# First FFN of a two-layer encoder: three pairs on unnormalised tokens, then three Strassen groups on normalised ones

## The chip, the cores and the metric

The kernel runs on one core of a Trainium2 chip. Five engines work beside each other, each with its own queue of instructions that it takes in order: TensorE (PE, matmuls and transposes; PEld is its loading of the stationary operand), VectorE (DVE), ScalarE (ACT), GpSimd (POOL) and SyncE (SP, which issues the DMAs). An instruction waits at the head of its queue until what it reads has been written and what it overwrites has been read. The metric is the device time of one execution in microseconds; the median of several runs is compared.

## The reference

Two layers. In each, a first FFN, a token mixer and a second FFN, each with a norm before it and one behind it. There are 256 tokens of width 1024; the FFN's hidden width is 2816. All arrays are float32. The change concerns the first FFN of the first layer alone:

```python
def rms_norm(x, g):
    xf = x.astype(jnp.float32)
    xf = xf * lax.rsqrt(jnp.mean(xf * xf, axis=-1, keepdims=True) + NORM_EPS)
    return (xf * g.astype(jnp.float32)).astype(x.dtype)

def swiglu(h, w_up, w_down):
    a, b = jnp.split(h @ w_up, 2, axis=-1)
    return (jax.nn.silu(a) * b) @ w_down

for l in range(DEPTH):
    h = rms_norm(x, ffn1_pre_g[l])
    x = x + 0.5 * rms_norm(swiglu(h, ffn1_w_up[l], ffn1_w_down[l]), ffn1_post_g[l])
    ...
```

## The kernel before

**Numbers.** Each float32 operand is held as two tiles of type float32r, a high part and the rest. ACT copies the high part (line 119 for weights, 164 for most others), DVE subtracts it from the original (lines 120 and 165). A product is then three matmuls, high by high, high by low and low by high (`mm3`, line 229).

**Weights.** They arrive in units of 128 x 2048 (1 MB) in the order in which they are used, through 5 buffers `raw` (line 57), and are split into 5 pairs of buffers `wh`, `wl` (line 58). `next_unit` (line 127) loads and splits; the first `FINE` = 5 units of a stage are split in four parts, later ones in two. So DVE and ACT can be some units ahead of PE, and no more.

**An FFN** (`ffn`, line 297). The hidden width is cut into 11 "pairs" of 256 gate and 256 value columns. An "up" of a pair (`up`, line 344) multiplies both halves of the tokens (c = 0, 1) by two units: 48 matmuls of 128 x 512. `swiglu` (line 334) makes silu(gate) times value from the PSUM bank; `turned` (line 320) transposes the outcome on PE and splits it into `hid`. A "down" (line 311) multiplies a pair's hidden tokens by one unit into four PSUM banks `acc`: 24 matmuls. `PLAN` (line 37) lists the order. The last three downs are done by `tail` (line 284) half by half of the tokens, so that the post-norm, the next stage's pre-norm and its transposes of the first half run beside the matmuls of the second.

**Two forms of FFN.** All FFNs but the first take normalised, transposed and split tokens, and beside them a float32 copy of the transposed tokens (`kept`, made in `pre_norm`, line 187). Their plan has six of the pairs in three "groups" (`group`, line 382): two pairs are made together by a Strassen-Winograd scheme, with 7 block products of 12 matmuls each in place of 8. It needs sums of token blocks (`token_sums`, line 372), sums of weight blocks (128 x 2048, `add` at line 364 on the `raw` tiles), 7 split units in place of 4, and sums of the products.

The first FFN of the first layer (`raw_rstd` given, line 431) has no stage before it in which x could be normalised. It takes x already transposed from memory, multiplies by the norm's gain while splitting (`first_tokens`, line 183), starts its matmuls at once, and multiplies by the reciprocal root mean square of each token where the result leaves PSUM (lines 337 and 338). Its plan has no groups: up and down of pairs 2 to 10 in turn.

**Other work in the first FFN.** `setup` (line 477) makes cosines, sines and the lambdas' sums for the mixers; `mem_scale` (line 568) takes the root mean squares of the 256 memory tokens; `mem_gain` (line 577) multiplies the transposed memory by its gain and splits it. In the first FFN these are issued behind down 2 (`n == 5`); in the other first FFN, that of layer 2, `mem_gain` is issued behind the whole plan, ahead of `tail`.

**What sets the order.** The program order sets priorities; a scheduler places each instruction into its engine's queue at compile time, ahead of earlier ones when those would wait. The order on each engine is then fixed. `issue_after` (line 137) demands an order between two instructions.

**Buffers the steps touch.** Tokens, sums of tokens and split memory share 2 tiles `xhl` (line 59); hidden and memory tiles share 12 (line 60); `s2` has 8 tiles of 512 (line 62), two of `gain` (line 63). PSUM has 4 banks `acc`, 2 `ma` and 2 `mb`; transposes go through `mb`.

Of the kernel before, what the change touches and what calls it, by code (L numbers as in the profile page):

```python
# [10 lines left out]
F32R = mybir.dt.float32r  # L11
# [6 lines left out]
P = 128  # L18
# [15 lines left out]
T_UP = 36  # L34
T_ROPE = 13
T_SC = (242, 336)
PLAN = [[(t[0], int(t[1:])) for t in plan.split()] for plan in (
    "u2 d0 u3 d1 u4 d2 u5 d3 u6 d4 u7 d5 u8 d6 u9 d7 u10",
    "u2 d0 g3 d1 d2 u5 d3 g6 d4 d5 u8 d6 g9 d7",
)]  # L40
T_KT = (200, 222)
T_DA = (186, 210, 278, 302)
T_PV = (193, 218, 285, 310)
# [8 lines left out]
def encoder_kernel(ctx, tc, x_d, xt_d, mem_d, memt_d, pos_d, w_d, gains_d, cols_d, lamv_d, poolw_d, cst_d, out_d):  # L52
# [6 lines left out]
    xts = ctx.enter_context(tc.tile_pool(name="xts", bufs=2))  # L59
# [17 lines left out]
    def t2(shape=(P, 512), dt=F32):  # L77
        return s2.tile(list(shape), dt, name="s2")
# [4 lines left out]
    x = [const.tile([P, D], F32, name=f"x{c}") for c in range(2)]  # L83
# [58 lines left out]
    def in_order(ins):  # L142
        for early, late in zip(ins, ins[1:]):
            issue_after([late], early)
# [18 lines left out]
    def split(ps, h, l):  # L163
        high = nc.scalar.copy(out=h, in_=ps)  # L164
        return high, nc.vector.tensor_tensor(out=l, in0=ps, in1=h.bitcast(F32), op=ALU.subtract)  # L165
# [131 lines left out]
    def ffn(i, xx, late, kept, g_post, finish, ahead, raw_rstd=None):  # L297
        fine[0] = FINE
        hid = {}
        acc = [[None, None], [None, None]]  # L300

        def lhs_of(c, kk, k):
            return hid[kk][0][:, c, k, :], hid[kk][1][:, c, k, :]
# [29 lines left out]

        def swiglu(p, c, ps):
            sg, hn = t2((P, S)), t2((P, S))
            if raw_rstd:
                nc.scalar.activation(out=sg, in_=ps[:, 0:S], func=AF.Silu, scale=raw_rstd[c])
                nc.vector.scalar_tensor_tensor(out=hn, in0=ps[:, S:2 * S], scalar=raw_rstd[c], in1=sg, op0=ALU.mult, op1=ALU.mult)
            else:
                nc.scalar.activation(out=sg, in_=ps[:, 0:S], func=AF.Silu)  # L340
                nc.vector.tensor_tensor(out=hn, in0=ps[:, S:2 * S], in1=sg, op=ALU.mult)  # L341
            turned(hn, c, [p])
# [20 lines left out]
        def add(out, a, b):  # L363
            nc.vector.tensor_tensor(out=out, in0=a, in1=b, op=ALU.add)  # L364

        if kept:
            sums = xts.tile([P, 2, 4 * 4, P], F32R, name="xhl")

            def summed(j):
                return lambda k: (sums[:, 0, 4 * j + k, :], sums[:, 1, 4 * j + k, :])  # L370

        def token_sums():
            a11, a12, a21, a22 = (kept[c, b] for c in range(2) for b in range(2))
            s1 = t2()
            nc.vector.tensor_tensor(out=s1, in0=a22, in1=a21, op=ALU.subtract)
            nc.vector.tensor_tensor(out=a21, in0=a11, in1=a21, op=ALU.subtract)
            nc.vector.scalar_tensor_tensor(out=a11, in0=s1, scalar=-1.0, in1=a11, op0=ALU.mult, op1=ALU.subtract)
            nc.vector.scalar_tensor_tensor(out=a12, in0=a11, scalar=-1.0, in1=a12, op0=ALU.mult, op1=ALU.subtract)
            for j, t in enumerate((s1, a11, a21, a12)):
                split(t.rearrange("p (k t) -> p k t", t=P), sums[:, 0, 4 * j:4 * j + 4, :], sums[:, 1, 4 * j:4 * j + 4, :])  # L380
# [47 lines left out]
            for c in range(2):  # L428
                swiglu(p, c, banks[c])

        if raw_rstd:
            ws = [(next_unit(), next_unit())]
            hs, ls = first_high, first_low
            (ha, la), (hb, lb), (hc, lc), (hd, ld) = (zip(*late[c, b]) for b in range(2) for c in range(2))
            in_order([*ha, *hs[0:4], *hb, *hc, hs[4], hs[5], *hd, *hs[6:8]])
            in_order([*la, *ls[0:4], *lb, *lc, ls[4], ls[5], *ld, *ls[6:8]])
            ws.append((next_unit(), next_unit()))
            for c in range(2):
                rstd_of(halves(x[c]), 1.0, None, raw_rstd[c])
            up_first(0, ws[0])  # L440
            for c in range(2):
                up(1, c, ws[1], acc_bank)
        else:
            ws = [(next_unit(), next_unit()) for _ in range(2)]
            done = []
            for c in range(2):
                for p in range(2):
                    done += up(p, c, ws[p])
            issue_after(late, done[T_UP])
            token_sums()  # L450
        for n, (what, p) in enumerate(PLAN[bool(kept)]):
            if what == "d":
                down(p)
            elif what == "u":
                up_both(p)
            else:
                group(p)
            if not kept and n == 5:
                ahead()
        if kept:  # L460
            ahead()
        todo = [(next_unit(), p) for p in range(NPR - 3, NPR)]
        return tail(acc, todo, lhs_of, 0, NPR - 1, g_post, True, finish, flush)

# [2 lines left out]
    rst = const.tile([P, 2], F32, name="rst")  # L467
# [377 lines left out]
    cur = xt_pair()  # L845
# [15 lines left out]
    late = {cb: first_tokens(*cb, xt[cb], cur) for cb in ((0, 0), (1, 0), (0, 1), (1, 1))}  # L861

    kept = None
    for i, (kind, l, row) in enumerate(stages):
        nx = {}

        def finish(c):
            if i + 1 == len(stages):
                for b in range(2):
                    fs = slice(b * 512, (b + 1) * 512)  # L870
                    nc.sync.dma_start(out=out_d[c * P:(c + 1) * P, fs], in_=x[c][:, fs])
                return []
            if c == 0:
                nx["xx"] = xt_pair()
                nx["kept"] = {} if stages[i + 1][0] == "ffn" else None
                nx["g"] = gain(stages[i + 1][1] * 10 + stages[i + 1][2])
            return pre_norm(c, halves(x[c]), nx["g"], nx["xx"], nx["kept"])()

        if kind == "ffn":
            def ahead():  # L880
                if i == 0:
                    setup()
                    mem_scale()
                if row == 0:
                    nx["mem"] = mem_gain(l)

            late = ffn(i, cur, late, kept, gain(l * 10 + row + 1), finish, ahead, [rst[:, c:c + 1] for c in range(2)] if i == 0 else None)
        else:
            late = mix(l, cur, late, mem, finish)
        cur, mem, kept = nx.get("xx"), nx.get("mem"), nx.get("kept")  # L890
# [24 lines left out]
def _pack(a, np):  # L915
    L = DEPTH
    units = []

    def cols(w, idx):
        units.append(np.ascontiguousarray(w[:, idx].reshape(KT, P, 256).transpose(1, 0, 2)).reshape(P, 2048))  # L920

    def block(w, half, col):
        units.append(np.ascontiguousarray(w[512 * half:512 * half + 512, col:col + 512].reshape(4, P, 512).transpose(1, 0, 2)).reshape(P, 2048))

    def wide(w, idx):
        both = w[:, idx]
        for half in range(2):
            block(both, half, 0)

    def rows(w, j):  # L930
        units.append(np.ascontiguousarray(w[256 * j:256 * (j + 1)].reshape(2, P, D).transpose(1, 0, 2)).reshape(P, 2048))

    def ffn(up, down, first):
        def pair(p):
            wide(up, np.r_[256 * p:256 * p + 256, D_FF + 256 * p:D_FF + 256 * p + 256])

        pair(0)
        pair(1)
        for what, p in PLAN[not first]:
            if what == "d":  # L940
                rows(down, p)
            elif what == "u":
                pair(p)
            else:
                for half, col in ((0, 0), (0, D_FF), (1, D_FF), (1, 0)):
                    block(up, half, 256 * p + col)
        for p in range(NPR - 3, NPR):
            rows(down, p)

    for l in range(L):  # L950
        ffn(a["ffn1_w_up"][l], a["ffn1_w_down"][l], l == 0)
        wi = a["w_in"][l]
        for s in (256, 768, 1280):
            wide(wi, slice(s, s + 512))
        for s in (0, 1792):
            cols(wi, slice(s, s + 256))
        wide(a["w_mem_kv"][l], slice(0, 512))
        for i in range(6):
            wide(a["w_gate"][l], slice(512 * i, 512 * i + 512))
        br = np.concatenate([a["w_br_pool"][l], a["w_br_da"][l], a["w_br_ca"][l]], axis=0)  # L960
        for i in range(2):
            wide(br, slice(512 * i, 512 * i + 512))
        for j in range(4):
            rows(a["w_out"][l], j)
        ffn(a["ffn2_w_up"][l], a["ffn2_w_down"][l], False)
    return np.stack(units)


# [39 lines left out]
```

## Time and profile before

| what | us |
|---|---|
| median of 3 runs (lowest to highest) | 1126.62 (1125.84 to 1129.25) |
| the profiled execution | 1127.05 |
| its span, first to last instruction | 1124.9 |
| busy: DVE, ACT, POOL | 893.5, 651.9, 26.1 |
| granted TensorE clock, mean | 0.997 |

Stages by the first matmul that PE takes from each: the first FFN from 6.97, its mixer from 195.2, the second FFN from 385.1, the next layer's first FFN from 565.7, its mixer from 747.2. HBM delivers 193 GB/s over the span; in the first 56 us it is 342 and 388 GB/s.

The page lists busy time for each engine, then shares of the span in 40 slices, the chain of work that ended last, and groups of instructions by source line. A row of the groups reads: line, engine, operation, tile written and tiles read, partitions x elements, type, count, then busy us, mean ns of one, and idle time of the engine ahead of them with what ended it. A row of the chain reads: start, length, engine, tile, line and count. A row of the timeline is the same with the operation named, and in brackets how long the engine had been idle and who released it. PE at 99% busy means that matmuls follow each other without a gap; it isn't a measure of how much they compute.

### The profile page before, as it was taken

What the parts mean: (1) busy time and instruction counts of PE and PEld (TensorE: products, weight loads), DVE (VectorE), ACT (ScalarE), POOL (GpSimd) and SP (SyncE); (2) the same over time, 40 slices, a digit from 0 to 9 for tenths busy, and PEclk for the clock granted to TensorE, in tenths of its full rate; (3) what the DMA queues carried; (4) which work ended last, traced back from release to release, by engine and by line L of the source; (5) the groups of instructions that cost most, each with busy time, mean ns of one, the idle gap of its engine ahead of it and who ended that gap; (6) DMA issues with size and microseconds to landing.
All of it is one profiled execution on the core that took longest, in us unless ns stands there. A gap on an engine that the chain in (4) does not pass through costs nothing.

```text
span 1124.9 us, 13897 instructions
## 1 busy us (share of the span) xinstructions
PE 1109.0 (99%) x5247; PEld 913.2 (81%) x5247; DVE 893.5 (79%) x1215; ACT 651.9 (58%) x1082; POOL 26.1 (2%) x37
## 2 busy tenths in 40 slices
PE   9999999999999999999999999999999999999997
PEld 6888888888888878888878888878887887888886
DVE  6767456657758889999989999995776687999994
ACT  7657355556575557475575664755566546574561
POOL 0000000000000100000000000010000001000000
PEclk9999999999999999999999999999999999999999
DMA  9965643554553554573851835666455634263831
GB/s 342 388 229 225 219 152 117 192 220 150 206 206 132 195 179 148 190 264 136 310 190 73 299 135 202 219 240 218 160 175 191 244 149 169 75 245 135 293 112 38
DMA packets 35489, 218.27 MB, mean 194 GB/s; under 512 B 4192, under 2 KB 4448, under 8 KB 11232
## 3 DMA queue, kind: packets, MB, share of 16 engines
q1 hardware_dynamic: 35424, 217.40, 53.4%
q8 instruction: 41, 0.67, 0.2%
q14 instruction: 24, 0.20, 0.1%
HBM read 216.33 MB, written 1.05 MB: 193 GB/s over the span
## 4 chain that ended last, share of the span: by engine, by line
PE 92%; DVE 4%; ACT 1%; DMA 1%; POOL 1%; issue 0%; SPq 0%; DVEq 0%; POOLq 0%; ACTq 0%
PE ma L235 52%; PE acc L277 23%; PE mb L235 8%; DVE wl L120 2%; PE acc L235 2%; PE mb L325 2%; POOL sm L148 1%; PE acc L663 1%; DMA hid<-in_memt 1%; PE acc L686 1%; PE mb L563 1%; DVE x L227 1%; DMA raw<-in_w 1%; PE acc L749 1%; ACT wh L119 0%; PE mb L207 0%
## 5 line engine op out<-in xcount | busy, mean ns | idle before, releaser
L120 DVE TENSOR_TENSOR wl<-raw,wh 128x1024 fp32r<-128x1024 f32 (+1 forms) x498 | 524.2, 1092 | 101.6 <-ACT wh L119 99.0
L235 PE MATMUL ma<-wh,xhl 128*128 128x512 f32 x1760 | 562.3, 394 | 1.1 <-ACT wh L119 1.1
L119 ACT CAST wh<-raw 128x1024 fp32r<-128x1024 f32 (+1 forms) x498 | 445.0, 948 | 197.9 <-PE ma L235 65.6
L235 PEld LDWEIGHTS ma<-wh,xhl 128*128 128x128 f32 x1760 | 330.3, 188 | 70.8 <-ACT wh L119 2.4
L235 PE MATMUL ma<-wl,xhl 128*128 128x512 f32 x880 | 346.3, 394 | 0.5 <-DVE wl L120 0.5
L277 PE MATMUL acc<-wh,hid 128*128 128x512 f32 x704 | 228.2, 395 | 0.0
L235 PEld LDWEIGHTS ma<-wl,xhl 128*128 128x128 f32 x880 | 165.8, 188 | 35.0 <-DVE wl L120 1.5
L277 PEld LDWEIGHTS acc<-wh,hid 128*128 128x128 f32 x704 | 132.2, 188 | 26.8
L277 PE MATMUL acc<-wl,hid 128*128 128x512 f32 x352 | 137.1, 391 | 0.0
L235 PE MATMUL mb<-wh,xhl 128*128 128x512 f32 x280 | 90.5, 389 | 0.0
L364 DVE TENSOR_TENSOR raw<-raw 128x2048 f32<-128x2048 f32 x36 | 82.4, 2288 | 0.4
L277 PEld LDWEIGHTS acc<-wl,hid 128*128 128x128 f32 x352 | 66.3, 188 | 12.7
L235 PEld LDWEIGHTS mb<-wh,xhl 128*128 128x128 f32 x280 | 52.6, 188 | 11.0
L340 ACT ACTIVATE s<-ma 128x256 f32<-128x256 f32 x30 | 11.2, 386 | 77.1 <-PE ma L235 77.1
L235 PE MATMUL mb<-wl,xhl 128*128 128x512 f32 x140 | 54.5, 389 | 0.0
L148 POOL TENSOR_TENSOR sm<-sm,mhalf 128x1 f32<-128x1 f32 (+1 forms) x26 | 23.2, 891 | 1009.8 <-DVE sm L157 830.3
L164 ACT CAST hid<-mb 128x256 fp32r<-128x256 f32 x88 | 32.5, 369 | 16.2 <-PE mb L325 13.3
L165 DVE TENSOR_TENSOR hid<-mb,hid 128x256 fp32r<-128x256 f32 x88 | 37.0, 420 | 5.4 <-ACT hid L164 5.0
L277 PE MATMUL acc<-wh,xhl 128*128 128x512 f32 x128 | 40.7, 394 | 0.0
L155 ACT ACTIVATE junk<-acc 128x512 bf16<-128x512 f32 x24 | 14.3, 597 | 43.7 <-PE acc L277 43.7
L325 PE MATMUL mb<-ident,s 128*128 128x128 f32 x176 | 30.7, 273 | 5.3 <-DVE s L341 5.3
L325 PEld LDWEIGHTS mb<-ident,s 128*128 128x128 f32 x176 | 23.1, 140 | 15.5 <-issue 6.5
(159 smaller groups left out, 832.9 us busy)
## 6 DMA issues: line engine op xcount, KB each, us to landing
raw<-in_w SPq DMA_DIRECT2D x189, 1024.0 KB, 4.9
gain<-in_gains SPq DMA_DIRECT2D x17, 512.0 KB, 4.7
raw<-in_w SPq DMA_DIRECT2D x8, 256.0 KB, 6.4
hid<-in_memt SPq DMA_DIRECT2D x8, 256.0 KB, 6.6
hid<-in_xt SPq DMA_DIRECT2D x4, 256.0 KB, 6.0
raw<-in_w SPq DMA_DIRECT2D x2, 512.0 KB, 6.3
x<-in_x SPq DMA_DIRECT2D x4, 256.0 KB, 6.7
hid<-in_mem SPq DMA_DIRECT2D x4, 256.0 KB, 7.3
```

The costliest lines, as they stand in the source:

```text
L119: high = nc.scalar.copy(out=h[:, cs], in_=raw[:, cs])
L120: low = nc.vector.tensor_tensor(out=l[:, cs], in0=raw[:, cs], in1=h.bitcast(F32)[:, cs], op=ALU.subtract)
L148: nc.gpsimd.tensor_tensor(out=r, in0=v, in1=mhalf[:, :n], op=ALU.pow)
L155: sq.append(nc.scalar.activation(out=junk, in_=h, func=AF.Square, scale=fold / 32.0, accum_out=s[:, i:i + 1]))
L164: high = nc.scalar.copy(out=h, in_=ps)
L165: return high, nc.vector.tensor_tensor(out=l, in0=ps, in1=h.bitcast(F32), op=ALU.subtract)
L227: nc.vector.scalar_tensor_tensor(out=x[c][:, fs], in0=ts[b], scalar=r, in1=x[c][:, fs], op0=ALU.mult, op1=ALU.add)
L235: done.append(nc.tensor.matmul(out=out, lhsT=lhsT, rhs=rhs, start=(first and i == 0), stop=(last and i == n - 1)))
L277: done.append(nc.tensor.matmul(out=banks[b], lhsT=a, rhs=ww[:, k, fs], start=(kk == first and k == 0 and i == 0), stop=(kk == last and k = ...
L325: nc.tensor.transpose(out=tp[:, u * P:(u + 1) * P], in_=hn[:, u * P:(u + 1) * P], identity=ident)
L364: nc.vector.tensor_tensor(out=out, in0=a, in1=b, op=ALU.add)
L563: ins.append(nc.tensor.transpose(out=tp[:, i * P:(i + 1) * P], in_=a[:, hh, kt * P:(kt + 1) * P], identity=ident))
```

## The change

The first FFN gets the plan of the other FFNs. Pairs 0, 1 and 2 are still made from the raw tokens. Behind up 2, x is normalised and transposed inside this FFN (`normalised`: a gain row is loaded, `pre_norm` runs for both halves and fills `kept`), the token sums are made, and the rest of the plan (three groups and the pairs 5 and 8) uses normalised tokens. `setup` is issued behind down 2, `mem_scale` and `mem_gain` behind the plan. The packing of the weights follows the new order.

```diff
-PLAN = [[(t[0], int(t[1:])) for t in plan.split()] for plan in (
-    "u2 d0 u3 d1 u4 d2 u5 d3 u6 d4 u7 d5 u8 d6 u9 d7 u10",
-    "u2 d0 g3 d1 d2 u5 d3 g6 d4 d5 u8 d6 g9 d7",
-)]
+PLAN = [(t[0], int(t[1:])) for t in "u2 d0 g3 d1 d2 u5 d3 g6 d4 d5 u8 d6 g9 d7".split()]
...
+        raw = raw_rstd is not None
...
         def swiglu(p, c, ps):
             sg, hn = t2((P, S)), t2((P, S))
-            if raw_rstd:
+            if raw:
...
-        if kept:
+        def normalised():
+            nonlocal xx
+            xx = xt_pair()
+            g = gain(0)
+            for c in range(2):
+                pre_norm(c, halves(x[c]), g, xx, kept)()
+
+        def summed(j):
+            return lambda k: (sums[:, 0, 4 * j + k, :], sums[:, 1, 4 * j + k, :])
+
+        def token_sums():
+            nonlocal sums
             sums = xts.tile([P, 2, 4 * 4, P], F32R, name="xhl")
...
-        for n, (what, p) in enumerate(PLAN[bool(kept)]):
+        for n, (what, p) in enumerate(PLAN):
             if what == "d":
                 down(p)
             elif what == "u":
                 up_both(p)
             else:
                 group(p)
-            if not kept and n == 5:
-                ahead()
-        if kept:
-            ahead()
+            if raw and n == 0:
+                raw = False
+                normalised()
+                token_sums()
+            if i == 0 and n == 4:
+                setup()
+        ahead()
...
             def ahead():
                 if i == 0:
-                    setup()
                     mem_scale()
                 if row == 0:
                     nx["mem"] = mem_gain(l)
 
-            late = ffn(i, cur, late, kept, gain(l * 10 + row + 1), finish, ahead, [rst[:, c:c + 1] for c in range(2)] if i == 0 else None)
+            late = ffn(i, cur, late, kept if i else {}, gain(l * 10 + row + 1), finish, ahead, [rst[:, c:c + 1] for c in range(2)] if i == 0 else None)
```

More of the change, by code (lines that the diff above doesn't have):

```diff
@@ L364, in add @@
             nc.vector.tensor_tensor(out=out, in0=a, in1=b, op=ALU.add)
-        if kept:
+        def normalised():
[8 more added lines that the diff above has]
+            nonlocal sums
             sums = xts.tile([P, 2, 4 * 4, P], F32R, name="xhl")
-            def summed(j):
-                return lambda k: (sums[:, 0, 4 * j + k, :], sums[:, 1, 4 * j + k, :])
-        def token_sums():
             a11, a12, a21, a22 = (kept[c, b] for c in range(2) for b in range(2))
@@ L429, in up_first @@
                 swiglu(p, c, banks[c])
-        if raw_rstd:
+        sums = None
+        if raw:
             ws = [(next_unit(), next_unit())]
@@ L931, in rows, with ffn @@
         units.append(np.ascontiguousarray(w[256 * j:256 * (j + 1)].reshape(2, P, D).transpose(1, 0, 2)).reshape(P, 2048))
-    def ffn(up, down, first):
+    def ffn(up, down):
         def pair(p):
@@ L938, in ffn @@
         pair(1)
-        for what, p in PLAN[not first]:
+        for what, p in PLAN:
             if what == "d":
@@ L950, in _pack @@
     for l in range(L):
-        ffn(a["ffn1_w_up"][l], a["ffn1_w_down"][l], l == 0)
+        ffn(a["ffn1_w_up"][l], a["ffn1_w_down"][l])
         wi = a["w_in"][l]
@@ L964, in _pack @@
             rows(a["w_out"][l], j)
-        ffn(a["ffn2_w_up"][l], a["ffn2_w_down"][l], False)
+        ffn(a["ffn2_w_up"][l], a["ffn2_w_down"][l])
     return np.stack(units)
```

## Prediction

> **What bounds the kernel now.** I read the page first, then busy time by stretches, the waits of PE, the chain in order of time, and the VectorE (DVE) timeline. Columns of the stretches: start and end, length, then busy us with counts for PE, PEld, DVE, ACT, POOL, the granted clock, DMA share, GB/s.
>
> ```profile
> PE 1109.0 (99%) x5247; PEld 913.2 (81%) x5247; DVE 893.5 (79%) x1215; ACT 651.9 (58%) x1082; POOL 26.1 (2%) x37
> core 0: us, PE busy (x) PEld busy (x) DVE busy (x) ACT busy (x) POOL busy (x), PEclk, DMA share, GB/s
> 10.30:195.20 184.90, 184.90 (x838) 151.97 (x839) 119.16 (x198) 106.77 (x184) 3.62 (x6) 1.00 0.65 242
> 565.70:747.20 181.50, 179.02 (x817) 147.51 (x816) 170.86 (x205) 112.86 (x173) 4.02 (x4) 1.00 0.53 192
> 655.70:703.40 47.70, 47.70 (x218) 39.39 (x217) 46.44 (x48) 29.16 (x37) 0.00 (x0) 1.00 0.54 199
> ```
>
> TensorE (PE) is busy 99% of the span, and in the first FFN (10.30 to 195.20) it is never idle; DVE there works 119.16 of 184.90 us. The FFN of 565.70 already has Strassen groups: PE is 3.4 us shorter, but DVE works 170.86 of 181.50 us. One of its cycles (a group of two pairs, then two downs, an up, a down) has DVE busy 46.44 of 47.70 us. So plain FFNs are held by PE alone, grouped ones by PE with DVE close behind: DVE has 1.3 us free in a cycle.
>
> **The change on PE.** A pair costs 48 matmuls, a group of two pairs 7 products of 12.
>
> ```profile
> 37.32 5.50 PE ma L235 x24
> 43.03 5.50 PE acc L277 x24
> 48.74 10.94 PE ma L235 x48
> 195.31 8.39 PE ma L235 x37
> 399.20 5.50 PE ma L235 x24
> 192.20 1.03 PE L207 MATMUL mb<-ident,s 128*128 128x128 f32 x8
> 192.99 0.48 PE L277 MATMUL acc<-wh,hid 128*128 128x512 f32 x1
> ```
>
> The chain gives 10.94/48 = 0.228 us a matmul. Three groups take 3 x 84 = 252 matmuls in place of 288: 36 x 0.228 = 8.2 us less. Normalising x adds 16 transposes; eight of them hold PE from 192.20 to 192.99, so 2 x 0.79 = 1.6 us more. Hidden-layer transposes stay 44. PE alone: 6.6 us less, 178.3 us in place of 184.9.
>
> **The change on DVE.** Rows of the groups by form, and one run of five:
>
> ```profile
> L120 DVE TENSOR_TENSOR wl<-raw,wh 128x1024 fp32r<-128x1024 f32 x378 | 448.3, 1221 | 89.0 <-ACT wh L119 86.7 <-issue 1.3 <-PE ma L235 0.4
> L364 DVE TENSOR_TENSOR raw<-raw 128x2048 f32<-128x2048 f32 x36 | 82.4, 2288 | 0.4
> L364 DVE TENSOR_TENSOR s<-s,mb 128x512 f32<-128x512 f32 x36 | 24.6, 685 | 1.8 <-PE mb L235 1.8
> L165 DVE TENSOR_TENSOR xhl<-s,xhl 128x512 fp32r<-128x512 f32 x12 | 8.2, 687 | 0.0
> L165 DVE TENSOR_TENSOR hid<-mb,hid 128x256 fp32r<-128x256 f32 x88 | 37.0, 420 | 5.4 <-ACT hid L164 5.0
> L194 DVE TENSOR_TENSOR s<-x,gain 128x512 f32<-128x512 f32 x20 | 12.8, 684 | 0.0
> L199 DVE TENSOR_SCALAR s<-s,sm 128x512 f32<-128x512 f32 x20 | 8.8, 484 | 2.7 <-POOL sm L148 2.7
> L338 DVE SCALAR_TENSOR_TENSOR s<-ma,rst,s 128x256 f32<-128x256 f32 x20 | 9.6, 481 | 20.6 <-ACT s L337 20.5
> 684.11 5.76 DVE L120 TENSOR_TENSOR wl<-raw,wh 128x1024 fp32r<-128x1024 f32 x5
> ```
>
> Five in 5.76 us with 1.22 each means 1.135 from start to start, 0.085 less than recorded; I take 0.085 off every row: 2.20 for a 2048-wide add, 0.60 for a 512-wide operation, 0.40 for L199 and L338, 0.335 for a hidden split. Added: 42 unit splits in place of 33, 18 halves x 1.135 = 20.4; 12 weight adds x 2.20 = 26.4; nine 512-wide steps in each group, 27 x 0.60 = 16.2; normalising, 4 x 0.60 (L194) + 4 x 0.40 (L199) + 4 x 0.60 (L165) + 0.25 = 6.65; token sums, 8 x 0.60 = 4.8. Removed: 12 L338, 4.8. Net 69.7 us. The recorded 119.2 counts the 0.085 for each of the 198 instructions that stands alone, up to 17 us in all, and none for those in runs; so the new sum lies between 172 and 189, and since the splits, the bulk, come in runs, I take **185 us of DVE work, where PE alone would take 178.3**. (The grouped FFN's 170.86 has no set-up and no raw tokens, and is of that order.) That is the core of my forecast: the saved matmuls are paid on an engine that hasn't this much room in this stretch.
>
> ACT gains about as many instructions, but at 106.77 of 184.90 us it has the room. DMA bytes grow by one 512 KB gain row.
>
> **Where it bites: before the first group.** The first group's splits can't start early, since DVE is busy with start-up until about 36.9.
>
> ```profile
> 0.00:10.30 10.30, 7.56 (x18) 2.66 (x18) 3.63 (x9) 5.29 (x11) 0.73 (x7) 1.00 0.70 222
> 0.00:36.86 36.86, 34.11 (x137) 24.32 (x138) 25.78 (x52) 26.32 (x57) 1.84 (x9) 1.00 0.93 359
> 33.36 3.50 DVE L120 TENSOR_TENSOR wl<-raw,wh 128x1024 fp32r<-128x1024 f32 x3
> 601.94 2.29 DVE L364 TENSOR_TENSOR raw<-raw 128x2048 f32<-128x2048 f32 x1
> 604.80 2.29 DVE L364 TENSOR_TENSOR raw<-raw 128x2048 f32<-128x2048 f32 x1
> 607.96 2.75 PE ma L235 x12
> 607.90:747.40 139.50, 138.44 (x630) 114.26 (x629) 134.58 (x153) 89.75 (x130) 2.01 (x2) 1.00 0.56 205
> 747.38 8.39 PE ma L235 x37
> ```
>
> At 36.86 the units of pairs 0 to 2 and of down 0 are split. From there DVE must do: two L338 and three hidden splits of pairs 1 and 2 (1.8), normalising (6.65), token sums (4.8): 13.25. Then two units of the group (4 x 1.135) and its first three weight adds (3 x 2.20): 11.1. It has this at 36.86 + 24.4 = 61.3. The grouped FFN has the same work done at 604.80 + 2.29 = 607.1, and its group begins on PE at 607.96, 0.9 later. So the group stands at 62.1 as the other does at its start. PE would be there at 48.74 + 1.6 = 50.3: DVE is **11.8 us late**, and PE waits about that much in and around the group.
>
> From its group to the mixer's first matmul the grouped FFN takes 747.38 - 607.96 = 139.4 us: 62.1 + 139.4 = 201.5.
>
> Corrections, with the rows they rest on:
>
> ```profile
> 80.58 0.42 DVE L485 TENSOR_TENSOR s<-s 128x256 f32<-128x256 f32 x1
> 88.05 0.18 DVE L522 COPY csd<-csd 128x16 f32<-128x16 f32 x1 [0.28 <-ACT csd L521]
> 725.75 7.41 DMA hid<-in_memt
> 730.75 1.71 ACT L175 ACTIVATE xhl<-hid,colt 128x256 fp32r<-128x256 f32 x4
> 733.19 1.71 ACT L175 ACTIVATE xhl<-hid,colt 128x256 fp32r<-128x256 f32 x4 [0.73 <-DMA hid<-in_memt]
> PE mb L207 <- DVE s L199: 1.1, 1, 1.1
> 14.24 27.33 SPq L104 DMA_DIRECT2D raw<-in_w  x10
> ```
>
> The set-up (cosines, lambdas), now behind down 2, is 26 small DVE instructions between the first two of these rows; without the splits and hidden work among them I take 4.6 us of the 7.7. Today idle DVE hides it. Then only what DVE has free behind the group does, 139.5 - 134.6 = 4.9 us, of which I count 3.4 as usable (2 x 1.3 in the cycles, 0.8 in the tail): 4.6 - 3.4 = +1.2 (bounds 0 and 4.6). Its three small loads on SP wait for nothing.
>
> The scaling and splitting of the memory moves from behind down 2 to the tail, where PE has 28 matmuls of cover for the norm between its two halves. The grouped FFN at 565.70 has the splitting half there: the load is in the chain for 7.41 us, ACT's L175 wait for it, the squares of the post-norm are queued behind them, and PE loses 1.1 us before its transposes; that is in the 139.4. Here four more 256 KB loads and four squares of the memory go in front, on SP also ahead of the tail's weight loads: +1.0 (bounds 0 and 7, a whole load).
>
> Against this, DVE is idle 36.86 - 25.78 = 11.1 us at the start, 6.7 of them before 10.30 and 4.4 behind. Once the new gain row has landed, normalising can use some; its load is queued among the weight loads that SP issues from 14.24 on, so late: -2.0 (bounds 0 and -4.4).
>
> Sum: 201.5 + 1.2 + 1.0 - 2.0 = 201.7 against 195.31, **6.4 us longer**. The profiled execution took 1127.05 (span 1124.9 and 2.15 around it; the median of the runs, 1126.62, is 0.4 less): 1127.05 + 6.4 = 1133. The check from the total: 185 us of DVE from 10.30 on end at 195.3 with no idle moment, at 199.7 with today's 4.4 idle us of the start, and later if DVE waits at all behind that. What follows is unchanged: the mixers start from a plain FFN (195.31 to 399.20) and from a grouped one (747.38 to 951.32), and each takes 203.9 us to the next chain entry of the FFN behind it.
>
> **A wait can also cost clock.**
>
> ```profile
> 950.90 0.41 PE L325 MATMUL mb<-ident,s 128*128 128x128 f32 x2 [1.99 <-DVE s L341]
> 951.32 7.07 PE ma L235 x24
> 951.30:955.00 3.70, 3.70 (x12) 2.84 (x11) 0.43 (x1) 0.37 (x1) 0.00 (x0) 0.56 0.81 283
> PE mb L325 <- DVE s L341: 5.3, 3, 2.0
> ```
>
> After a wait of 1.99 us the granted clock is 0.56, and 24 matmuls take 7.07 in place of 5.50: 1.6 us. The other two waits of this kind (5.3 us in all, the longest 2.0) cost none that shows: behind the first, the 24 matmuls at 399.20 take 5.50. In the new first group PE will wait several times. I cost it at nothing, because DVE paces there and a slow matmul runs in DVE's time; up to three drops (4.8 us) are the bound. The Trainium skill ("TensorE: Matmul & The Clock Gate", section "Why this matters for your kernels") warns only of PE gaps over some 3 us. By that rule waits of 2 us would cost no clock and the sum would stay; the row above shows one that did cost it.
>
> **The rivals.**
> - *Faster: start-up idle swallows the new work.* DVE's idle 11.1 us before 36.86 nearly equal the 11.8 us of lateness. If normalising and the first splits go there, the group starts at 50.3 and the mixer at 50.3 + 139.4 = 189.7, plus 0 to 3 for set-up and memory: 1121.5 to 1124.5. It breaks even at about 9 us recovered. For it: the list of PE's waits has none at a group of the other FFNs. Against: the 6.7 before 10.30 come when neither gain row nor weights are there.
> - *About even.* The 4.4 idle us are all used and the set-up costs nothing: 201.5 - 4.4 + 0 to 1 = 197 to 198, some 2 to 3 us longer: 1128 to 1130. The group's own slack in the other FFN (unknown, 0 to 2 us) helps here.
> - *Worse: waits in a row.* Clock drops (up to 4.8) and a memory load that holds ACT in the tail (up to 7) come on top of the forecast: 1138 to 1145.
>
> **How the numbers follow.** My forecast (1130.0 to 1138) has 0.55, about even (with the slack, 1125 to 1130) 0.23, the worse case 0.12, the faster one 0.10. A measurement of this kernel can tell 0.3%, 3.4 us, from no change: under 1123.2 lie 0.08 (most of the faster case), within 0.25, over 1130.0 lie 0.67. The range 1123.5 to 1142 leaves out most of the faster case and about half of the worse one.
>
> **What would show it.** In the new profile: DVE busy 9 in every tenth from some 25 us on; waits of PE on L120, L364 or the token splits between 42 and 80 us, 8 to 12 us in all, and none elsewhere but in the tail; 20 PE instructions fewer; the mixer's first matmul near 202. The forecast is wrong if PE starts the first group before 55 us and runs it through in 19, or if DVE shows idle stretches over 1 us between 37 and 75.

## The result, and the profile after

The changed kernel takes **1141.4 us** (median of 6 runs, 1138.82 to 1145.01), the kernel before 1126.95 beside it (1125.84 to 1129.25): a ratio of 1.0128, 95% interval 1.0113 to 1.0143. So it is 14.5 us slower, where 6.4 were forecast. The profiled spans are 1139.7 and 1124.9 us. Line numbers below are those of the changed kernel; matmuls are L232 (ups and groups) and L274 (downs), weight splits L116 (ACT) and L117 (DVE), sums L362, transposes of normalised tokens L204. In runs that add a plan of their own (`PLAN0`) each of these stands one line lower in the file: L233, L275, L117, L118, L363, L205.

The page of the changed kernel, busy time by engine and the row of VectorE (DVE) by fortieths of the span (28.5 us each):

```profile
PE 1112.8 (98%) x5227; PEld 911.4 (80%) x5227; DVE 959.6 (84%) x1282; ACT 675.4 (59%) x1116; POOL 28.2 (2%) x39
DVE  6999999767766879999979999996676678899994
```

20 PE instructions fewer, as worked out, and DVE at 9 from 28 to 200 us: the first FFN has become DVE's. DVE's busy time grew by 66.1 us (893.5 before), where 69.7 were forecast. What PE waits for, from 40 to 70 us, from 70 to 97, and from 145 to 235 (total, times, longest):

```profile
PE mb L232 <- DVE wl L117: 2.3, 1, 2.3
PE mb L232 <- ACT wh L116: 1.5, 1, 1.5
PE ma L232 <- ACT wh L116: 1.5, 1, 1.5
...
PE ma L232 <- ACT wh L116: 1.5, 1, 1.5
PE mb L232 <- DVE wl L117: 1.3, 1, 1.3
...
PE ma L232 <- DVE wl L117: 2.1, 1, 2.1
PE mb L204 <- DVE s L196: 1.3, 1, 1.3
```

The first five, 8.0 us, lie in the first group; none lies in the second and third, and from 97 to 145 us there is no wait at all. The waits aren't the whole loss. Busy time in stretches of 5 us (columns as in the prediction; the granted clock is the third figure from the end), and three rows of the timelines of PE and DVE:

```profile
55.00:60.00 5.00, 2.75 (x9) 1.75 (x7) 4.99 (x6) 1.24 (x2) 0.00 (x0) 0.82 0.00 0
60.00:65.00 5.00, 2.06 (x5) 0.95 (x4) 5.00 (x4) 3.85 (x4) 0.00 (x0) 0.50 0.00 0
65.00:70.00 5.00, 5.00 (x17) 3.92 (x16) 3.34 (x5) 3.92 (x5) 0.00 (x0) 0.65 0.26 72
70.00:75.00 5.00, 4.67 (x21) 3.55 (x19) 5.00 (x5) 0.00 (x0) 0.00 (x0) 1.00 0.33 138
75.00:80.00 5.00, 2.51 (x7) 1.82 (x8) 5.00 (x7) 4.88 (x6) 0.00 (x0) 0.87 0.74 262
80.00:85.00 5.00, 5.00 (x19) 3.95 (x19) 3.83 (x6) 4.01 (x5) 0.00 (x0) 0.79 0.92 329
```

```profile
58.10 0.69 PE L232 MATMUL mb<-wl,xhl 128*128 128x512 f32 x1 [2.25 <-DVE wl L117]
69.25 0.69 DVE L362 TENSOR_TENSOR s<-s,mb 128x512 f32<-128x512 f32 x1 [1.66 <-PE mb L232]
82.40 0.69 DVE L362 TENSOR_TENSOR s<-s,mb 128x512 f32<-128x512 f32 x1 [1.06 <-PE mb L232]
```

After the wait of 2.25 us PE's clock falls to 0.50; it is back at 1.00 from 70 to 75 us and falls again behind the waits of 1.54 and 1.27 us. The slow products take so long that DVE in its turn waits for PE, twice. The chain of the changed kernel, in order of time:

```profile
65.03 4.19 PE mb L232 x11
77.99 4.38 PE mb L232 x11
82.36 2.54 PE ma L232 x11
...
190.17 0.20 ACT junk L152
...
190.38 0.33 SPq L589
...
190.76 7.92 DMA raw<-in_w
...
213.67 3.01 PE ma L232 x12
216.68 0.87 PE mb L204 x8
...
412.21 7.13 PE ma L232 x24
```

Eleven matmuls take 4.19 and 4.38 us where the next eleven take 2.54. The group goes on PE from 50.70 to 84.74, 34.0 us, where its 84 matmuls at 0.228 are 19.2: **14.85 us lost**. In the tail SP can issue the last load of the transposed memory (L589) only at 190.38, behind a square of ACT (L152); the weights stand behind it, a weight's transfer is in the chain for 7.92 us, and PE waits 2.1 us in the mixer. Behind the mixer a clock drop (7.13 for 24 matmuls, 5.50 before) costs 1.6. That one is chance; the wait ahead of it is the same in both kernels, first before, then with the change:

```profile
398.79 0.41 PE L325 MATMUL mb<-ident,s 128*128 128x128 f32 x2 [1.95 <-DVE s L341]
411.80 0.41 PE L323 MATMUL mb<-ident,s 128*128 128x128 f32 x2 [1.96 <-DVE s L339]
```

As a mark for the runs below I use the second eight token transposes, which before come 8.4 us into the mixer, since they stand in every chain. Before:

```profile
203.70 0.87 PE mb L207 x8
```

With the change they come at 216.68, 13.0 later.

| run | median us | ratio to before (95%) | mark |
|---|---|---|---|
| the change | 1141.4 | 1.0128 (1.0113 to 1.0143) | 216.68 |
| only the first group | 1145.51 | 1.0166 (1.015 to 1.0183) | 222.43 |
| first group later | 1144.87 | 1.016 (1.0143 to 1.0177) | 220.51 |
| no weight sums in the first group | 1129.0 | 1.0013 (1.0004 to 1.0023) | 205.31 |
| idle matmuls in the first group | 1137.74 | 1.0098 (1.0076 to 1.012) | 214.55 |
| normalising early | 1137.28 | 1.0097 (1.007 to 1.0124) | 214.16 |
| no groups | 1137.31 | 1.0089 (1.0072 to 1.0107) | 214.36 |
| normalising alone | 1130.04 | 1.0029 (1.0019 to 1.0038) | 207.28 |
| memory in the tail alone | 1131.56 | 1.0041 (1.0027 to 1.0055) | 208.15 |
| memory scaling early | 1141.92 | 1.013 (1.0113 to 1.0147) | 217.65 |
| two groups | 1124.53 | 0.9977 (0.9965 to 0.9988) | 202.77 |
| two groups, memory early | 1124.63 | 0.9987 (0.9976 to 0.9998) | 201.05 |

One of the four runs without groups took 1237.32 us at a granted clock of 0.85; the median given is that of the other three (1137.65 with it), and the mark is from one more run of the same kernel, 1140.87 us.

### The profile page after: what moved, and what is told of

Read it like the earlier page. It is cut to its first block, busy times and chain, and to the rows that moved or that the text cites. A ratio compares the mean times of both kernels' runs of the same rounds, so it can differ in the third digit from the quotient of the medians.

```text
span 1139.7 us, 13968 instructions
## 1 busy us (share of the span) xinstructions
PE 1112.8 (98%) x5227; PEld 911.4 (80%) x5227; DVE 959.6 (84%) x1282; ACT 675.4 (59%) x1116; POOL 28.2 (2%) x39
## 4 chain that ended last, share of the span: by engine, by line
PE 86%; DVE 6%; ACT 3%; DMA 2%; POOL 1%; issue 1%; SPq 0%; DVEq 0%; POOLq 0%; ACTq 0%
PE ma L232 47%; PE acc L274 21%; PE mb L232 11%; DVE wl L117 3%; PE mb L323 2%; DMA raw<-in_w 2%; PE acc L232 1%; ACT wh L116 1%; POOL sm L145 1%; DVE x L224 1%; PE acc L671 1%; PE acc L694 1%; PE mb L571 1%; DVE raw L362 1%; DMA hid<-in_xt 1%
## 5 line engine op out<-in xcount | busy, mean ns | idle before, releaser
L117 DVE TENSOR_TENSOR wl<-raw,wh 128x1024 fp32r<-128x1024 f32 (+1 forms) x516 | 544.7, 1093 | 67.9 <-ACT wh L116 65.4
L116 ACT CAST wh<-raw 128x1024 fp32r<-128x1024 f32 (+1 forms) x516 | 462.1, 950 | 193.3 <-DVE raw L362 85.5
L232 PE MATMUL ma<-wh,xhl 128*128 128x512 f32 x1664 | 534.9, 395 | 3.1 <-ACT wh L116 3.0
L232 PEld LDWEIGHTS ma<-wh,xhl 128*128 128x128 f32 x1664 | 313.1, 189 | 70.5 <-ACT wh L116 5.1
L232 PE MATMUL ma<-wl,xhl 128*128 128x512 f32 x832 | 328.6, 395 | 2.1 <-DVE wl L117 2.1
L274 PE MATMUL acc<-wh,hid 128*128 128x512 f32 x704 | 227.7, 395 | 0.0
L232 PEld LDWEIGHTS ma<-wl,xhl 128*128 128x128 f32 x832 | 157.4, 189 | 36.1 <-DVE wl L117 4.0
L274 PEld LDWEIGHTS acc<-wh,hid 128*128 128x128 f32 x704 | 132.3, 188 | 26.8
L274 PE MATMUL acc<-wl,hid 128*128 128x512 f32 x352 | 137.7, 393 | 0.0
L232 PE MATMUL mb<-wh,xhl 128*128 128x512 f32 x352 | 117.4, 400 | 1.5 <-ACT wh L116 1.5
L362 DVE TENSOR_TENSOR raw<-raw 128x2048 f32<-128x2048 f32 x48 | 109.6, 2284 | 0.4
L232 PEld LDWEIGHTS mb<-wh,xhl 128*128 128x128 f32 x352 | 68.0, 194 | 17.2 <-ACT wh L116 2.2
L274 PEld LDWEIGHTS acc<-wl,hid 128*128 128x128 f32 x352 | 66.2, 188 | 13.1 <-DVE wl L117 0.6
L232 PE MATMUL mb<-wl,xhl 128*128 128x512 f32 x176 | 70.6, 401 | 3.5 <-DVE wl L117 3.5
L161 ACT CAST hid<-mb 128x256 fp32r<-128x256 f32 x88 | 32.5, 369 | 23.6 <-PE mb L323 19.2
L232 PEld LDWEIGHTS mb<-wl,xhl 128*128 128x128 f32 x176 | 34.0, 193 | 11.5 <-DVE wl L117 4.5
L274 PE MATMUL acc<-wh,xhl 128*128 128x512 f32 x128 | 40.7, 394 | 0.0
L152 ACT ACTIVATE junk<-acc 128x512 bf16<-128x512 f32 x24 | 14.3, 596 | 38.9 <-PE acc L274 38.9
L362 DVE TENSOR_TENSOR s<-s,mb 128x512 f32<-128x512 f32 x48 | 32.6, 679 | 4.8 <-PE mb L232 4.8
```

The costliest lines, as they stand in the source:

```text
L116: high = nc.scalar.copy(out=h[:, cs], in_=raw[:, cs])
L117: low = nc.vector.tensor_tensor(out=l[:, cs], in0=raw[:, cs], in1=h.bitcast(F32)[:, cs], op=ALU.subtract)
L152: sq.append(nc.scalar.activation(out=junk, in_=h, func=AF.Square, scale=fold / 32.0, accum_out=s[:, i:i + 1]))
L232: done.append(nc.tensor.matmul(out=out, lhsT=lhsT, rhs=rhs, start=(first and i == 0), stop=(last and i == n - 1)))
L274: done.append(nc.tensor.matmul(out=banks[b], lhsT=a, rhs=ww[:, k, fs], start=(kk == first and k == 0 and i == 0), stop=(kk == last and k = ...
```

## The experiments

**Where the first group stands.** The theory: the group comes before DVE is through with its preparation, and PE loses that lateness. First, the group one up and one down later, in the first FFN alone:

```diff
+PLAN0 = [(t[0], int(t[1:])) for t in "u2 d0 u5 d1 g3 d2 d5 d3 g6 d4 u8 d6 g9 d7".split()]
...
-        for n, (what, p) in enumerate(PLAN):
+        for n, (what, p) in enumerate(PLAN if i else PLAN0):
...
-            if i == 0 and n == 4:
+            if i == 0 and n == 5:
                 setup()
```

> The first FFN alone runs its plan as u2 d0 u5 d1 g3 d2 d5 d3 g6 d4 u8 d6 g9 d7: the same work, but an up and a down (16.4 us of PE) stand between the normalising and the first group; the setup stays behind down 2. Theory A (the first group comes before VectorE is through with its preparation; the price is that lateness, 14.85 us of the 14.8 net): VectorE has the group ready at 63.05 + 3 units x 2.27 = 69.9, PE is there at 50.7 + 16.4 = 67.1, so the lateness falls to some 3 to 5 us, waits of PE between 45 and 95 us to under 3 us, the mixer's first matmul comes at 194 to 197 (205.66 with the change), the time is 1129 to 1133. Rival N (normalising and transposing x in the middle of the FFN is what costs, wherever the group stands): the loss stays, mixer at 204 to 206, 1139 to 1143. Rival C (the price is the memory work in the tail and the mixer behind it): 1139 to 1143 too, with the first group free of waits.

Measured: 1144.87, above what any of the theories gave. Chain, and PE's waits from 97 to 145 us:

```profile
68.63 2.74 PE ma L233 x12
...
94.56 1.82 PE acc L275 x8
```

```profile
PE ma L233 <- ACT wh L117: 3.1, 1, 3.1
PE mb L233 <- ACT wh L117: 1.6, 1, 1.6
PE mb L233 <- DVE wl L118: 0.8, 1, 0.8
```

The first group now takes 25.9 us (94.56 - 68.63) in place of 34.0. With its up moved ahead, though, only three downs stand between it and the second group; DVE is late there too, 5.5 us of new waits, where the change has none, and that group takes 29.0 us (111.69 to 140.71). Against 19.2 for 84 matmuls the two lose 6.8 and 9.9 us, more together than the 14.85 of the change. The edit moved the lateness and made more of it, so it doesn't decide between the theories. The next one does: the first group where it was, and plain ups in place of the other two. Here and in the runs below, where the plan changes, only the new plan is shown; it is put to use as above.

```diff
+PLAN0 = [(t[0], int(t[1:])) for t in "u2 d0 g3 d1 d2 u5 d3 u6 d4 u7 d5 u8 d6 u9 d7 u10".split()]
...
```

> The first FFN alone runs u2 d0 g3 d1 d2 u5 d3 u6 d4 u7 d5 u8 d6 u9 d7 u10: the first of the three groups stays where the change puts it, the other two are plain ups again, so VectorE has about 42 us less to do behind it; memory work in the tail as in the change. Theory P (the place: the first group comes 12 to 14 us before VectorE is through, and what PE loses there doesn't come back): the group's loss is that of the change, the time is the run without groups, 1137.65, less 12 matmuls (2.7 us), plus 10 to 14.9: 1145 to 1150. Rival S (the sum: VectorE's work of three groups overfills the FFN, wherever they stand): the loss shrinks with the two groups that are gone, 1134 to 1139.

Measured: 1145.51, where P gave 1145 to 1150 and S 1134 to 1139. Chain, and busy time from 97 to 145 us:

```profile
50.66 0.68 PE ma L233 x3
...
84.61 1.82 PE acc L275 x8
```

```profile
97.00:145.00 48.00, 48.00 (x218) 39.56 (x217) 31.81 (x53) 22.57 (x33) 0.00 (x0) 1.00 0.67 239
```

The group takes 33.95 us as in the change, though DVE is busy only 31.81 of 48 us behind it. So it is the **place**, not the sum over the FFN: PE never gets back what it lost, and two groups fewer make the kernel slower still.

**What fills the group.** The four sums of weight blocks left out in that group:

```diff
-            add(w11, w11, w12)
+            if i or p > 3:
+                add(w11, w11, w12)
...
```

> As the change, but the four sums of weight blocks (128x2048, 2.2 us of VectorE each, 8.8 in all) of the first group in the first FFN alone are left out, so its output is not the reference's; every matmul, split and transfer stays. Theory A: VectorE is 4 to 8.8 us earlier in that group, and the clock drops behind its waits shrink with them: the group's 34.0 us fall to 23 to 28, the time to 1130 to 1135. Rival N or C: the group gets little shorter, the time stays at 1138 to 1142. Rival D (a slow clock is most of the price and one wait is enough to set it off): half of the gain or less, 1136 to 1139, with the granted clock still under 0.8 between 55 and 70 us.

Measured: 1129.0, 12.4 us less than the change for 8.8 us of DVE; better than any theory had it. Busy time from 60 to 65 us:

```profile
60.00:65.00 5.00, 5.00 (x24) 4.10 (x23) 5.00 (x7) 4.26 (x5) 0.00 (x0) 1.00 0.62 210
```

PE is busy in all of this stretch at clock 1.00, where the change had 2.06 us at 0.50. DVE's work in this group is the cause, and the clock adds to it. With the sums goes also the order that the splits must wait for them; the run doesn't separate the two, and both are what the sums cost.

**The clock alone.** Idle matmuls ahead of three products of the first group (`fill` is 1 there and 0 elsewhere), into the bank that the product overwrites:

```diff
+        def busy(bank, n, after):
+            for _ in range(n if i == 0 else 0):
+                issue_after([nc.tensor.matmul(out=bank, lhsT=xx[0][:, 0, 0, :], rhs=xx[0][:, 0, 0:4, :], start=True, stop=True)], after[-1])
...
+            fill = p == 3
...
-            product(d, summed(0), split_unit(w11, 2))
+            busy(d, 8 * fill, done)
+            done = product(d, summed(0), split_unit(w11, 2))
```

> As the change, with 28 idle matmuls of 128x512 (6.4 us at full clock) in the first group of the first FFN, 8 ahead of its second product, 12 ahead of the third and 8 ahead of the sixth, each into a bank that the product behind it overwrites; the outcome is unchanged. They stand where PE waited 2.25, 1.48, 1.47, 1.54 and 1.27 us and the granted clock fell to 0.5. Theory A (VectorE alone paces the group, a slow clock costs nothing, as the prediction had it): the group gets no shorter, the time stays at 1140 to 1144. Rival D (the slow clock is a price of its own, since VectorE waits for PE's slow products too, 1.66 and 1.06 us): the granted clock in 55 to 85 us rises over 0.95, VectorE's two waits go, the group's 34.0 us fall by 3 to 5 although PE has more to do, the time is 1136 to 1139.

Measured: 1137.74, 3.7 us less than the change (0.4 to 6.4 by the two intervals), with 6.4 us more for PE to do. Busy time in two stretches, and PE's timeline:

```profile
60.00:65.00 5.00, 3.26 (x15) 2.38 (x14) 5.00 (x4) 3.55 (x4) 0.00 (x0) 1.00 0.00 0
75.00:80.00 5.00, 3.74 (x16) 2.88 (x16) 5.00 (x6) 5.00 (x7) 0.00 (x0) 1.00 0.81 295
```

```profile
64.55 0.50 PE L232 MATMUL ma<-wh,xhl 128*128 128x512 f32 x1 [1.74 <-ACT wh L116]
81.67 0.39 PE L274 MATMUL acc<-wh,hid 128*128 128x512 f32 x1
```

The clock is 1.00 in every stretch of 5 us from 50 to 85, DVE works through its part of the group in the same order and has no idle time from 60 us on, and the group takes 30.7 us (51.01 to 81.67) in place of 34.0. That is rival D, and its size: of the loss some 3 to 4 us are clock, the rest is DVE's.

**The start.** The gain row loaded behind x, and the normalising issued behind pair 0:

```diff
         load_x(c)
+    g_first = gain(0)
...
             up_first(0, ws[0])
+            new = normalised()
```

> As the change, but the gain row of the new normalising is loaded right behind x, and x is normalised and transposed behind pair 0 in place of behind up 2, so that VectorE can do this in the 4.4 us that it is idle between 10.3 and 36.9 us; the same instructions in all. With the change the normalising ran at 35.0 to 39.9 us and won nothing of this idle time, where the prediction counted 2.0 (0 to 4.4). If the idle time can be had: VectorE has the first group's units and sums 2 to 4.4 us ahead of 63.05, the group's 34.0 us shrink to 30 to 32, the time is 1136 to 1139.5. If the start is held by the weights' loads (DMA share 0.95 until 36.9), what is put in front pushes the splits of pairs 1 and 2 back, PE waits for them before 43 us, and the time stays at 1140 to 1144.

Measured: 1137.28, 4.1 us less than the change (0 to 7 by the two intervals, so its size rests on the trace). Chain:

```profile
55.51 4.41 DVE raw L362 x2
...
62.30 5.06 PE mb L232 x11
```

The two sums of weight blocks end at 59.9 in place of 63.05. So DVE's idle time at the start can be had. The edit moved the load of the gain row and the place of the normalising together, so which of the two kept the work out of the idle time in the change isn't shown. The clock still falls (5.06 for 11 matmuls).

**Normalising and memory without groups.** The old plan, normalised tokens from up 3 on, memory work in the tail:

```diff
+PLAN0 = [(t[0], int(t[1:])) for t in "u2 d0 u3 d1 u4 d2 u5 d3 u6 d4 u7 d5 u8 d6 u9 d7 u10".split()]
...
-                pre_norm(c, halves(x[c]), g, xx, kept)()
+                pre_norm(c, halves(x[c]), g, xx, None)()
...
                 normalised()
-                token_sums()
```

> The first FFN alone runs the old plan without groups, but x is normalised and transposed behind up 2, setup stands behind down 2 and the memory's scaling and splitting behind the plan, as in the change; the float32 copy of the tokens and the token sums are left out. The outcome is what the change costs without its groups. Theory A: 16 transposes (1.7), the start (0.5), the tail (1 to 2) and the mixer behind it (2.5): 1131 to 1134; PE has no wait over 1 us between 45 and 160 us. Rival N: waits of PE between 42 and 60 and 1137 or more. Rival C: as A in the sum, but with the waits in the tail and the mixer, over 5 us there.

Measured: 1137.31, over the 1131 to 1134 that A and C gave, and at N's 1137. So its two parts were run apart, first the normalising with the memory work where it was, then the memory work moved with no normalising, both with the plan without groups, and the whole once more for its trace.

```diff
                 setup()
-        ahead()
+                ahead()
+        if i:
+            ahead()
```

> The kernel before with one part of the change: x is normalised and transposed behind up 2 and the rest of the first FFN uses it; no groups, no token sums, and setup, memory scaling and splitting behind down 2 as before. The run without groups came out at 1137.65, 4 to 6 us over what was expected; this run and the next split it. Theory A: 16 transposes (1.7 us) and the start (0.5), 1128.5 to 1130. Rival N (normalising in the middle is the 10 us): 1134 to 1138, with PE waiting between 42 and 60 us.

```diff
-            if raw and n == 0:
-                raw = False
-                normalised()
-                token_sums()
```

> The kernel before with another part of the change: memory scaling and splitting behind the plan, in the tail; setup stays behind down 2; no normalising, no groups. Theory A: the tail and the mixer behind it lose what they lost with the change (1.1 + 2.5), 1129.5 to 1132. Rival C (the memory in the tail is the price of the run without groups, 1137.65): 1134 to 1137, with over 5 us of waits in the tail or at the mixer's start.

> The run without groups once more, for its trace: the profile of the first run shows a clock of 0.85 over the whole span and can't be laid beside the others. Its parts measured alone give 3.4 (normalising) and 4.9 us (memory in the tail), 1135 in all, against 1137.65 measured. If the parts add up, the second eight token transposes of the mixer come at 203.70 + 3.6 + 4.5 = 211.8 and a clock drop behind makes up the rest; if they don't, they come at 213 or later, with a longer wait in the tail.

Measured: normalising alone 1130.04, memory alone 1131.56, by the ratios 3.3 and 4.6 us. That is no 10 us for normalising in the middle, so N falls; in the whole, too, PE has no wait between 40 and 60 us. The sum of the parts, 7.9, and the 10.0 of the whole agree only within the intervals, and at the mark they don't add up (214.36, where 211.8 would be the sum). The second run of the whole shows what differs: PE's waits for the normalised tokens in the tails of both layers, first in it, then in the run of memory alone. The longest of each, 4.7 and 3.0, is in the tail of the first FFN; what is left, 3.0 and 1.1, is in layer 2, where before has 1.1.

```profile
PE mb L205 <- DVE s L197: 7.6, 2, 4.7
```

```profile
PE mb L205 <- DVE s L197: 4.0, 2, 3.0
```

The chain of the run with memory alone tells why:

```profile
179.06 5.83 DMA hid<-in_mem
...
186.61 1.88 ACT xhl L173 x5
188.49 0.04 issue
188.53 1.30 ACT xhl L173 x3
189.82 0.58 ACT junk L153 x2
...
196.99 1.94 PE mb L205 x8
```

ScalarE (ACT) waits for the memory's load, takes its four squares and eight splits, and only then the squares of the post-norm (189.82), for which DVE and then PE wait; eight transposes then take 1.94 us in place of 0.87, at a clock of 0.50 (197 to 200 us). In the run without groups two loads stand one behind the other in the chain (5.36 and 5.75 us). The cost of the memory in the tail is a matter of when its loads land: 4.5 us at the mark in one, about 7 in the other (over the run with normalising alone).

With the change itself, the memory's scaling behind down 3:

```diff
                 setup()
+            if i == 0 and n == 6:
+                mem_scale()
...
-                if i == 0:
-                    mem_scale()
```

> As the change, but the memory's scaling (four loads of 256 KB, four squares) stands behind down 3 in place of behind the plan; the splitting of the memory stays in the tail. Theory C (memory loads ahead of the tail's weights on SP are what costs in the tail and the mixer: 1.1 + 2.5 us): the mixer's wait of 2.1 us at 213.7 goes, the first mixer takes 204 in place of 206.5, the time falls by 2 to 3.5, to 1138 to 1139.5. Against C: within 1 us of 1141.4, and the mixer waits as before, since VectorE comes late from the groups.

Measured: 1141.92, no gain, where C gave 2 to 3.5 us. Busy time from 97 to 145 us:

```profile
97.00:145.00 48.00, 46.02 (x207) 37.43 (x207) 46.02 (x68) 31.23 (x47) 1.10 (x2) 1.00 0.55 207
```

The mixer's wait falls from 2.1 to 0.85 us, as C has it, but PE now waits 2 us in the stretch of the second group, where it waited for nothing before the four squares and their loads were put there. So the run shows that the scaling has a part in the mixer's wait, and not what it costs in all.

**Two groups.** Pairs 3 and 4 by plain ups, groups 6 and 9 kept.

```diff
+PLAN0 = [(t[0], int(t[1:])) for t in "u2 d0 u3 d1 u4 d2 u5 d3 g6 d4 d5 u8 d6 g9 d7".split()]
...
```

> The first FFN alone runs u2 d0 u3 d1 u4 d2 u5 d3 g6 d4 d5 u8 d6 g9 d7: x is normalised and transposed behind up 2 as in the change, pairs 3 and 4 are made by plain ups, and only two groups are left, the first of them 66 us of PE later. Theory A: no lateness at all; PE does 24 matmuls less than before (5.5 us) and 16 transposes more (1.7), so the mixer's first matmul comes at 192 to 194, and with what the tail and the mixer lost (1.1 + 2.5) and a chance clock drop of 1.6 behind it the time is 1126 to 1130, about even with before. Rival N (normalising in the middle costs some 10 us by itself): mixer at 202 or later, 1137 or more. Rival C (tail and memory): the first mixer takes 206 us or more in place of 203.9, whatever the first FFN does.

Measured: 1124.53, faster than before by 0.23% (0.12 to 0.35) and than the change by some 17 us. The mixer's first matmul comes at 193.83, where A had it (its time was 1.5 us too long), and not at N's 202 or later. Busy time of the two stretches in which the change lost its time:

```profile
36.86:68.00 31.14, 31.14 (x151) 25.78 (x150) 30.11 (x42) 22.54 (x35) 0.00 (x0) 1.00 0.72 262
68.00:97.00 29.00, 29.00 (x130) 23.63 (x128) 23.25 (x41) 13.93 (x19) 0.00 (x0) 1.00 0.43 167
```

PE is never idle, and DVE has 5.75 us free in the second stretch. Then also the memory's scaling behind down 2, and the loads of the transposed memory behind up 8:

```diff
                 setup()
+                mem_scale()
+            if i == 0 and n == 11:
+                mem_early.extend(mem_load())
...
```

> The run with two groups (1124.53), and beside it the memory's scaling behind down 2, where no group is near, and the four loads of the transposed memory behind up 8; only the splitting of the memory is left in the tail. Theory C2 (in a tail that VectorE and ScalarE reach in time, the memory's loads and squares ahead of the post-norm's squares on ScalarE are the 4.5 us that the run with the memory alone lost): the second eight token transposes of the mixer come 1.5 to 4 us earlier (202.77 with two groups), the time is 1121 to 1123. Against it: within 1 us of 1124.5, as in the run of the change with the scaling moved, where what the tail won was lost in the groups.

Measured: the mark at 201.05, 1.7 us earlier as forecast, but 1124.63 where 1121 to 1123 were, no gain that can be told. These two are the fastest kernels of the study, and equal.

## Why the prediction was wrong

The direction and the main mechanism held: DVE late before the first group, by its own work, with the loss never made up (the run with only that group), while the later groups have no waits. One sign of being wrong that the prediction named came true: DVE has an idle stretch of over 1 us between 37 and 75, the 1.66 us up to 69.25 in which it waits for a slow product. The step that failed shows in it, DVE pacing the group alone. The sum was 8.4 us short, by its steps, on the spans:

- **PE alone, -6.6.** Held: 20 instructions fewer, and two groups are faster than before. PE stood at the group at 50.7 to 50.9 in place of 50.3, 0.5 more.
- **DVE 11.8 us late, and 2.0 won at the start.** This was the term that failed: 9.8 forecast, 14.85 measured, 5.05 too little. Two assumptions made it.
  - **Clock drops "at nothing, because DVE paces there and a slow matmul runs in DVE's time".** The idle matmuls took 3.4 us off the group and 3.7 off the time. DVE didn't pace alone: the group is a row of hand-overs, sums wait for products (1.66 and 1.06 us in DVE's timeline) as products wait for splits, so the slow product was paid. The bound of 4.8 that I kept held it.
  - **Start-up idle "-2.0".** Nothing was won; the normalising ran at 35.0 to 39.9 us. The idle time was real, as the run with it early shows (sums ready 3.1 us sooner, 4.1 us off the time), but the normalising that is issued behind up 2 didn't get to use it; why, stays open. The lateness without clock, 14.85 less 3 to 4, is near 11.8, with no credit.
- **139.4 us from the group to the mixer, set-up +1.2, memory +1.0.** 141.6 forecast, 140.0 measured, 1.6 too much: PE waits for nothing between 78.0 and 202.2, so the set-up was hidden.
- **The mixers, 203.9 us behind a plain FFN and behind a grouped one, taken as unchanged.** 2.5 us too little: the tail's weights came late behind the memory's loads (7.92 us in the chain), and the mixer took the delay into its first products. The run with the scaling moved away supports this (0.85 us of wait left), but the run with two groups has the same memory work in its tail and no such wait, so it takes more than the memory's place. By itself, the memory in the tail costs 4.6 us (3.0 to 6.2 by the interval). I had looked for its price only in the tail.
- **Nothing behind the mixer.** The clock drop there, 1.6 us, was put at nothing, and the bound of 4.8 was for the new group alone; it is chance, and 0.35 is left over.

These are 0.5 + 5.05 - 1.6 + 2.5 + 1.95 = 8.4, with 6.4 the 14.8 of the spans. The rival "worse: waits in a row" named both mechanisms, clock drops and memory loads, and its 1138 to 1145 holds the result, though the memory cost its time in the mixer and not in the tail; I gave it 0.12 since I priced the clock by whether DVE was busy, and not by who waits for the slow product. Normalising alone cost 3.3 us, of which the transposes are 1.7; the rest (the start, and a clock of 0.95 until 36.9 us in its profile) wasn't settled. Nor was it settled why the run without groups cost more than its two parts, 10.0 against 7.9 us, if it did.

In the first group a wait of 2.25 us was followed by a clock of 0.50, two waits of 1.48 and 1.47 us kept it there, and behind two of 1.54 and 1.27 us it fell to 0.87 and 0.79. The Trainium skill ("TensorE: Matmul & The Clock Gate", section "Why this matters for your kernels") warns of idle gaps of PE over some 3 us between bursts of matmuls. This trace lost clock behind shorter ones.

## What to carry to other kernels

A saving on the bound engine that is bought on the second one must be checked where the second one is furthest behind, not over the stage: here the same change with its first group left out is faster than before, and with only that group it is slower than with all three. Where TensorE and a second engine hand over to each other in turn, a slow clock was paid although the second engine was the busier one, so look at both queues before a drop is put at nothing; idle matmuls in the waits paid here. Work moved into a tail is priced by what it stands ahead of in each queue, here ScalarE's squares and SP's weight loads, and by the stage behind.

## What the runs showed of the hardware

More work on PE made the kernel faster: 28 idle matmuls, 6.4 us of them, took 3.7 us off. With them a wait of 1.74 us left the clock at 1.00, and without them it was 0.50 in the stretch that holds waits of 1.48 and 1.47 us. Removing 8.8 us of DVE work took 12.4 us off, with the clock at 1.00 in that stretch.

The length of a single wait doesn't tell whether it costs clock. Ahead of the second FFN PE waits 1.94 to 1.99 us in each of the thirteen profiles behind the marks above, that of the kernel before among them; behind it 24 matmuls take 7.06 to 7.13 us in five of them (the change, the late group, two groups, normalising alone, memory scaling early) and 5.48 to 5.50 in the other eight. The drop in the first group, with five waits in a row, came back: 0.50 from 60 to 65 us also in the runs with only the first group and with memory scaling early.
